# A hybrid encoder layer's FFN: weight loads set ahead of frame loads, frame loads one pair at a time, form stores on another queue, spare blocks for the last forms, later transposes

## The chip, the core and the metric

The kernel runs on one core of one Trainium2 chip. The metric is the device time of one execution in microseconds, as the median of several runs. The engines are named as the profile names them: PE (TensorE, matrix products) with its weight loads PEld, DVE (VectorE), ACT (ScalarE), POOL (GpSimd) and SP (SyncE, which here only issues DMAs). DMAs are issued from SP's queue and from POOL's.

## The reference

One layer of a streaming encoder is run over 512 prompt frames and 64 frames of a running stream, 576 frames in all, with a model width of 2048 and an inner width of the feed-forward part (FFN) of 5632. Everything is float32.

```python
hn = rmsnorm(x, g_norm1)
proj = hn @ w_in                        # split into q, k, v, gb, gc, hc
...                                     # stick-breaking attention and a short convolution
mix = concatenate([rmsnorm(o_attn, g_attn_out), rmsnorm(o_conv, g_conv_out)])
x = x + mix @ w_out
h2 = rmsnorm(x, g_norm2)
x = x + (silu(h2 @ w_gate) * (h2 @ w_up)) @ w_down
```

Outputs are the new x for prompt and sample frames, the new key and value rows, and the convolution's state.

## The kernel before

**Numbers.** A float32 product is made of three matmuls on float32r halves: weights and frames are split in a high part and a low part, and high x high, low x high and high x low are summed. A matmul takes a 128 x 128 weight tile as the stationary operand and 288 frames (half of the 576) as the moving one. A *step* is three such matmuls.

**Stages.** The first 985 us or so hold the norms, the input projection with attention and convolution, the output projection, and the first gate and up block of the FFN, computed plainly by `wide`: for each of two weight tiles (kk) four blocks (j, i) of 24 matmuls, j the column tile, i the half of the frames. The two halves of the frames lie in different tiles; the one in `b12h` and `b12l` shares its memory with the weight buffer `raw_b`, whose first loads therefore wait until `wide` has read these tiles for the last time.

**Units of seven products.** The rest of the FFN is cut into *units*, each a product of 2 x 2 blocks computed with seven products instead of eight (a Strassen-Winograd scheme). Units 0 to 41 make gate and up for the feature pairs fp = 1 to 21; each has m = 8 steps per product. The units from NGU = 42 on are the down projection: the table `DOWN` lists *visits* (d, a, b), where d is one of eight output column pairs, and the pairs a to b of hidden features are added, m = b − a steps per product. The four accumulator blocks of a d are made at its first visit (`take_blocks`) and put out at its last.

**Weights.** `load_columns` (L1020) issues weight loads on SP whenever a buffer is free: the buffer A (`raw_a`) and B (`raw_b`) have two halves each, and a visit with m over 4 needs both halves of one of them. `prepare(n, p_)` splits the weight block of product p_ of unit n into one of four slots `whl`: a cast on ACT (L211), a subtraction on DVE (L212), and on DVE the sums of weights (L1082, L1094). After product 3 or 4 a buffer is free, and `prepare` calls `load_columns`.

**Running a product.** `run` multiplies (L1112), copies a partial result out of PSUM with ACT (`part`, L1122) and adds it up on DVE and POOL (L1137, L1142, L1144). For gate and up, `finish` (L959 to L966) makes silu(gate) x up and `put_forms` makes the seven *forms* of a feature pair, the frame side of the down projection. Each form is split by `put_form` into a tile with tag `hl` (two buffers) and stored to `hid_dram` by a DMA on POOL (L924): 22 x 7 = 154 stores of 288 KB.

**Frames of the down projection.** `load_pair` brings one feature pair (7 forms, 2 MB) from `hid_dram` back into one of seven places, on SP: one DMA (L1236, tiles `h_s` or `t`), or seven of 288 KB (L1228, tile `t`) for two of the places. `turned` says after which product of the last up unit the pairs 0 to 6 are called, and `down_calls` after which visit the later ones are: as soon as the pair that holds a place is used by all eight d. Several pairs can be called at once: 7 to 10 behind one visit, 11 to 13 behind another.

**Output.** At a d's last visit `store_y` spawns a coroutine per block: it waits for 4 steps of the product loop, transposes the block on PE into PSUM (`pot`, L1257), copies it back with DVE (L1259) and ACT (`obs`, two buffers, L1261), waits 5 more steps and issues the stores on SP (L1248, L1250, L1264).

**Order.** `order` lists the products of all units, two units woven into each other. The main loop calls `prepare` of the product three places ahead (`AHEAD = 3`), then `run`, then `load_pair` for what is due. From the last up unit on (NGU − 1) ACT, DVE, SP and POOL keep the program's order; ahead of it a scheduler sets the order of their instructions. SP, ACT, DVE, POOL and PE each work in order: an instruction that waits holds all behind it.

```python
if k_ + AHEAD < len(order):
    prepare(*order[k_ + AHEAD])
run(n, p_)
for p in turned.get((n, p_), calls[n - NGU] if n >= NGU and p_ == 4 else ()):
    load_pair(p)
```

Of the kernel before, what the change touches and what calls it, by code (L numbers as in the profile page):

```python
# [10 lines left out]
F32 = mybir.dt.float32  # L11
F32R = mybir.dt.float32r
# [29 lines left out]


DOWN = (
# [5 lines left out]
)  # L50


# [41 lines left out]
def tile_hybrid_stream_step(  # L94
# [743 lines left out]
    def h2(kt, i):  # L838
        if i == 0:
            return h2a[kt]  # L840
        return b22s[kt // 2] if kt % 2 else (b12h[:, kt // 2, :], b12l[:, kt // 2, :])
# [47 lines left out]
    def ps_tile(name):  # L889
        turn[0] += 1  # L890
        if turn[0] % 2:
            return ps_pj.tile([P, HALF], F32, tag="pj", name=name)
        return ps_z.tile([P, 512], F32, tag=f"z{turn[0] // 2 % 3}", name=name)[:, :HALF]
# [23 lines left out]
    gates = {}  # L917
    hid = {}

    def put_form(fp, n, src):  # L920

        t = tmp.tile([P, 2, HALF], F32R, tag="hl", name="form")
        split(t[:, 0], t[:, 1], src)
        nc.gpsimd.dma_start(out=hid_dram[fp][2 * n - 2 : 2 * n].rearrange("f p t -> p f t"), in_=t.bitcast(F32))  # L924

    def put_forms(fp, c, i):

# [23 lines left out]
    def finish(kind, fp, c, i, ps, part=None):  # L951

        a, b = HALVES[i]
        if kind == "gate":
            s = gates[c, i] = tmp.tile([P, HALF], F32, tag="r" if i else "y", name="gs")
        else:
            s = tmp.tile([P, HALF], F32, tag="sq", name="ut") if c == i else h2pool.tile([P, HALF], F32, tag="hx", name="ux", bufs=2)
        if part is None:
            nc.vector.tensor_tensor(out=s, in0=ps, in1=R2[:, a:b], op=ALU.mult)  # L959
        else:  # L960
            nc.vector.tensor_tensor(out=s, in0=ps, in1=part, op=ALU.add)  # L961
            nc.vector.tensor_tensor(out=s, in0=s, in1=R2[:, a:b], op=ALU.mult)
        if kind == "gate":
            nc.scalar.activation(out=s, in_=s, func=AF.Silu)
            return
        nc.vector.tensor_tensor(out=s, in0=s, in1=gates.pop((c, i)), op=ALU.mult)  # L966
        hid.setdefault(fp, {})[c, i] = s
        put_forms(fp, c, i)

    def wide(kind, hold=None):  # L970

        pss = {}
        for kk in range(2):
            whi, wlo = next_weight()
            for j in range(2):
                for i in range(2):
                    if kk == 0:
                        pss[j, i] = ps_tile("pw")
                    for k in range(8):
                        xh, xl = h2(8 * kk + k, i)  # L980
                        for n, (w_, x_) in enumerate(((whi, xh), (wlo, xh), (whi, xl))):
                            mm(pss[j, i], w_[:, k, j * P : (j + 1) * P], x_,
                               start=(kk == 0 and k == 0 and n == 0), stop=(kk == 1 and k == 7 and n == 2))
                        pipe.tick()
                    if kk == 1:
                        finish(kind, 0, j, i, pss[j, i])
            if hold and kk == 0:
                hold()

# [203 lines left out]

    def take_blocks(d):

        if d == 0:
            down["z"] = h2pool.tile([P, 6, HALF], F32, tag="z", name="acc_z")
        if d in (0, 3):
            four = [down["z"][:, q, :] for q in (range(4) if d == 0 else range(4, 6))]
            if d:  # L1200
                ax = down["pool"].tile([P, 2, HALF], F32, name="ax")
                four += [ax[:, q, :] for q in range(2)]
        elif d < 3:
            pool, tag = (tpool, "t12z") if d == 1 else (ypool, f"y{NP - 1}")
            t = pool.tile([P, 4, HALF], F32, tag=tag, name=f"acc{d}")
            four = [t[:, q, :] for q in range(4)]
        elif d < 6:
            four = [pool.tile([P, HALF], F32, tag=tag, name=f"acc{d}", bufs=2)
                    for pool, tag in (((tmp, "y"), (tmp, "r")) if d == 4 else ((tmp, "sq"), (h2pool, "hx")))
                    for _ in range(2)]  # L1210
        else:
            pool, tag = (tmp, "hl") if d == 6 else (rpool, "R")
            two = [pool.tile([P, 2, HALF], F32, tag=tag, name=f"acc{d}", bufs=2) for _ in range(2)]
            four = [t[:, q, :] for t in two for q in range(2)]
        for q, ap in enumerate(four):
            acc[d, q // 2, q % 2] = ap

    def add_residual(d):
        for c in range(2):
# [3 lines left out]
    def load_pair(p):  # L1223
        q = p % SLOTS
        if q in (3, 6):
            slots[p] = [t34[f][:, q // 6] for f in range(FORMS)]
            for f in range(FORMS):
                nc.sync.dma_start(out=slots[p][f].bitcast(F32),  # L1228
                                  in_=hid_dram[p][2 * f : 2 * f + 2].rearrange("f p t -> p f t"))
            return  # L1230
        if q in (2, 4):
            t = t12[:, 1 - q // 4].rearrange("p j f t -> p (j f) t")
        else:
            t = h2s[q // 5][:, SB * (q % 5) : SB * (q % 5 + 1), :]
        slots[p] = [t[:, 2 * f : 2 * f + 2, :] for f in range(FORMS)]
        nc.sync.dma_start(out=t.bitcast(F32), in_=hid_dram[p].rearrange("f p t -> p f t"))  # L1236

    def store_y(n, c, i):

        d = UNITS[n][1]  # L1240
        src, cs, f0 = acc[d, c, i], slice((2 * d + c) * P, (2 * d + c + 1) * P), HALVES[i][0]
        r = HALF - 2 * P

        def put(f, ap):

            rows, n_p = ap.shape[0], max(min(TP - f, ap.shape[0]), 0)
            if n_p:
                nc.sync.dma_start(out=yp[f : f + n_p, cs], in_=ap[:n_p])  # L1248
            if n_p < rows:
                nc.sync.dma_start(out=ys[f + n_p - TP : f + rows - TP, cs], in_=ap[n_p:])  # L1250

        def work():
            yield 4
            po = misc("pot")[:, : 3 * P]
            for q in range(3):
                w = min(P, HALF - q * P)
                nc.tensor.transpose(po[:w, q * P : (q + 1) * P], src[:, q * P : q * P + w], ident)  # L1257
            ob = src[:, : 2 * P].rearrange("p (i c) -> p i c", c=P)
            nc.vector.tensor_copy(out=ob, in_=po[:, : 2 * P].rearrange("p (i c) -> p i c", c=P))  # L1259
            obs = down["pool"].tile([r, P], F32, tag="obs", name="obs", bufs=2)  # L1260
            nc.scalar.copy(out=obs, in_=po[:r, 2 * P :])  # L1261
            yield 5
            if i == 0:
                nc.sync.dma_start(out=yp[: 2 * P, cs].rearrange("(i p) c -> p i c", p=P), in_=ob)  # L1264
            else:
                put(f0, ob[:, 0, :])
                put(f0 + P, ob[:, 1, :])
            put(f0 + 2 * P, obs)

        pipe.spawn(work())  # L1270


    turned = {(NGU - 1, 2): (0, 1), (NGU - 1, 6): (2,), (NGU - 1, 7): (3,), (NGU - 1, 5): (4,),
              (NGU - 1, 3): (5,), (NGU - 1, 4): (6,)}
    mode = ExitStack()
    AHEAD = 3
    for k_ in range(AHEAD):
        prepare(*order[k_])
    for k_, (n, p_) in enumerate(order):
        if (n, p_) == (NGU - 1, 1):  # L1280
            mode.enter_context(tc.manual_schedule(engines={mybir.EngineType.Activation, mybir.EngineType.DVE,
                                                           mybir.EngineType.SP, mybir.EngineType.Pool}))
            down["pool"] = tc.alloc_tile_pool(name="dpool", bufs=1, reuse_waits="tile", side="left")
        if k_ + AHEAD < len(order):
            prepare(*order[k_ + AHEAD])
        run(n, p_)
        for p in turned.get((n, p_), calls[n - NGU] if n >= NGU and p_ == 4 else ()):
            load_pair(p)
        if p_ == 2:
            for d in residual.get(n, ()):  # L1290
                add_residual(d)
    pipe.flush()
    mode.close()
    down["pool"].release()
# [35 lines left out]
```

## Time and profile before

| | |
|---|---|
| median of 3 runs | 2501.8 us (2500.9 to 2502.32) |
| the profiled execution | 2507.3 us, its span 2505.6 us |
| granted TensorE clock, mean | 0.991 of full speed |
| PE busy | 2442.1 us, 97% of the span |
| DVE busy | 1752.2 us, 70% |
| ACT busy | 1075.8 us, 43% |
| POOL busy | 348.1 us, 14% |
| moved by DMA | 336.51 MB, 134 GB/s as a mean |

The profile is of one execution, and its times count from the start of the span. In rows of an engine's timeline the columns are the start and the length in us, the engine, the line of the kernel, the operation, what is written from what is read, the shape, how often, and in square brackets how long the engine sat idle before it and what released it. `A <- B: 9.6, 3, 4.6` in a list of waits says that A waited for B 9.6 us in total, 3 times, 4.6 us at most. A DMA row with a median at its end gives the KB of one transfer and the microseconds from issue to landing.

### The profile page before, as it was taken

The page shows a single profiled execution, that of the slowest core. Times are in us where ns is not written, and L with a number is a line of the kernel's source. Part 1 is how long each engine was busy: PE and PEld are TensorE (multiplying, and loading weights), DVE is VectorE, ACT ScalarE, POOL GpSimd, SP SyncE. Part 2 cuts the span into 40 slices and gives each one's busy share as a digit, 9 for nine tenths or more (in the row PEclk, how much of TensorE's full clock was granted, in tenths as well). Part 3 has the DMA queues.
Part 4 walks back from the last instruction along what each step waited for, and adds up shares of the span by engine and source line. Part 5 has one row for each costly group of instructions (what it writes and reads, how often), then busy time and mean ns, then how long its engine had stood idle before and what let it go on. Part 6 is the DMA issues. An engine that isn't in the chain of part 4 may idle for free. (4 is left out here: it accounts for less than half of the span.)

```text
span 2505.6 us, 44203 instructions
## 1 busy us (share of the span) xinstructions
PE 2442.1 (97%) x18137; PEld 2425.9 (97%) x18137; DVE 1752.2 (70%) x2701; ACT 1075.8 (43%) x1917; POOL 348.1 (14%) x490
## 2 busy tenths in 40 slices
PE   8999999999999999999999999999999898999997
PEld 8999999999999999999999999999999898999897
DVE  7766666353345557888888888888887777777775
ACT  5655565231132345444444444444443443344333
POOL 2111010110020120001011010110101003421211
PEclk9999999999999999999999999999999899999999
DMA  8232323222242333444445444454447637765532
GB/s 260 82 96 86 90 78 88 75 85 85 85 160 85 101 129 117 134 134 137 133 149 154 132 135 136 149 153 129 137 137 245 217 124 202 213 185 187 175 109 66
DMA packets 436339, 336.51 MB, mean 134 GB/s; under 512 B 10222, under 2 KB 418920, under 8 KB 436136
## 3 DMA queue, kind: packets, MB, share of 16 engines
q1 hardware_dynamic: 419208, 283.53, 37.6%
q0 software_dynamic: 16928, 50.15, 6.2%
q8 instruction: 142, 2.33, 0.4%
q14 instruction: 61, 0.50, 0.1%
HBM read 269.33 MB, written 64.31 MB: 133 GB/s over the span
## 5 line engine op out<-in xcount | busy, mean ns | idle before, releaser
L1112 PE MATMUL psy<-t,whl 128*128 128x288 f32 x2916 | 445.4, 298 | 11.4 <-ACT part L1122 9.6
L203 PE MATMUL pj<-xhi,whi 128*128 128x288 f32 x1504 | 451.7, 300 | 0.0
L203 PE MATMUL pj<-xlo,whi 128*128 128x288 f32 x1504 | 445.9, 297 | 1.7 <-DVE xlo L337 1.7
L203 PE MATMUL pj<-xhi,wlo 128*128 128x288 f32 x1504 | 445.5, 296 | 0.0
L1112 PE MATMUL psy<-h_s,whl 128*128 128x288 f32 x2724 | 419.4, 298 | 16.4 <-ACT part L1122 15.7
L1112 PEld LDWEIGHTS psy<-t,whl 128*128 128x128 f32 x2916 | 410.0, 191 | 14.2 <-ACT part L1122 10.8
L1112 PEld LDWEIGHTS psy<-h_s,whl 128*128 128x128 f32 x2724 | 383.6, 191 | 18.8 <-ACT part L1122 17.0
L1112 PE MATMUL psw<-t,whl 128*128 128x288 f32 x2592 | 380.9, 297 | 0.0
L212 DVE TENSOR_TENSOR whl<-raw_a,whl 128x1024 fp32r<-128x1024 f32 (+5 forms) x288 | 303.0, 1052 | 83.2 <-ACT whl L211 81.9
L1112 PEld LDWEIGHTS psw<-t,whl 128*128 128x128 f32 x2592 | 358.8, 190 | 0.0
L211 ACT CAST whl<-raw_a 128x1024 fp32r<-128x1024 f32 (+5 forms) x288 | 255.3, 894 | 142.4 <-DVE raw_a L1082 50.2
L203 PEld LDWEIGHTS pj<-xlo,whi 128*128 128x128 f32 x1504 | 285.1, 190 | 2.0 <-DVE xlo L337 2.0
L203 PEld LDWEIGHTS pj<-xhi,whi 128*128 128x128 f32 x1504 | 285.4, 190 | 0.4
L203 PEld LDWEIGHTS pj<-xhi,wlo 128*128 128x128 f32 x1504 | 285.3, 190 | 0.5 <-DVE wlo L167 0.2
L212 DVE TENSOR_TENSOR whl<-raw_b,whl 128x1024 fp32r<-128x1024 f32 (+5 forms) x198 | 195.2, 987 | 96.1 <-ACT whl L211 94.9
L211 ACT CAST whl<-raw_b 128x1024 fp32r<-128x1024 f32 (+5 forms) x198 | 163.2, 835 | 190.1 <-issue 72.7
L166 ACT CAST whi<-raw_a 128x1024 fp32r<-128x1024 f32 (+1 forms) x138 | 140.0, 1031 | 232.7 <-PE pj L203 95.8
L924 POOL DMA_DIRECT2D hid_dram<-form x154 | 112.5, 731 | 903.0 <-DVE form L212 756.2
L1122 ACT COPY part<-psy 128x288 f32<-128x288 f32 x243 | 96.8, 398 | 236.1 <-PE psy L1112 234.6
L167 DVE TENSOR_TENSOR wlo<-raw_a,whi 128x1024 fp32r<-128x1024 f32 (+1 forms) x132 | 160.2, 1226 | 24.0 <-ACT whi L166 22.7
L1112 PE MATMUL psx<-h_s,whl 128*128 128x288 f32 x1122 | 168.8, 299 | 6.0 <-DVE gs L961 6.0
L1112 PEld LDWEIGHTS psx<-h_s,whl 128*128 128x128 f32 x1122 | 157.4, 192 | 6.2 <-issue 6.2
(357 smaller groups left out, 3700.9 us busy)
## 6 DMA issues: line engine op xcount, KB each, us to landing
raw_a<-in_w_in_dram SPq DMA_DIRECT2D x47, 1024.0 KB, 5.6
hid_dram<-form POOLq DMA_DIRECT2D x154, 288.0 KB, 2.8
raw_a<-in_w_gate_dram SPq DMA_DIRECT2D x23, 1024.0 KB, 5.8
raw_a<-in_w_up_dram SPq DMA_DIRECT2D x23, 1024.0 KB, 6.0
raw_b<-in_w_gate_dram SPq DMA_DIRECT2D x21, 1024.0 KB, 7.1
raw_b<-in_w_up_dram SPq DMA_DIRECT2D x21, 1024.0 KB, 7.3
h_s<-hid_dram SPq DMA_DIRECT2D x10, 2016.0 KB, 12.6
raw_a<-in_w_out_dram SPq DMA_DIRECT2D x16, 1024.0 KB, 5.4
```

The source lines that it names most:

```text
L166: nc.scalar.copy(out=hi[:, a:b], in_=raw[:, a:b])
L167: lo_eng.tensor_tensor(out=lo[:, a:b], in0=raw[:, a:b], in1=hi[:, a:b].bitcast(F32), op=ALU.subtract)
L203: mm(ps, w_[:, k, csl], x_[:, k, a:b], start=(k == 0 and n == 0), stop=(k == nk - 1 and n == 2))
L211: nc.scalar.copy(out=hi, in_=src)
L212: (lo_eng or nc.vector).tensor_tensor(out=lo, in0=src, in1=hi.bitcast(F32), op=ALU.subtract)
L924: nc.gpsimd.dma_start(out=hid_dram[fp][2 * n - 2 : 2 * n].rearrange("f p t -> p f t"), in_=t.bitcast(F32))
L1112: mm(ps, whl[:, w_, j, :], x_, start=(start and j == 0 and q == 0), stop=(j == len(xs_) - 1 and q == 2), skip_group_check=True)
L1122: nc.scalar.copy(out=t, in_=st["y"])
```

## The change

- `AHEAD` goes from 3 to 4, and `run` now comes ahead of `prepare` in the main loop; `load_pair` still comes last.
- Pairs that are due go into a list. One is issued at a time, and only when enough steps have passed since the last: 8 for the pairs 0 and 1, 16 for the other ones in the last gate and up units, `PACE` = 20 in the down projection.
- Form stores go to SP's queue for all feature pairs but the last. The last pair's stay on POOL's, and its forms 5, 7, 6 and 4 are put into four spare blocks (`ax`, two of `t`, one of `z`), which `take_blocks` uses as accumulators later, instead of the `hl` tiles.
- `wide` runs its four blocks with the other half of the frames (i = 1) first.
- The table `DOWN` is another one, with 38 visits instead of 39. The last visits of the eight d have m = 5, 5, 3, 5, 3, 3, 4, 3; before they had 7, 7, 5, 3, 3, 3, 4, 6.
- `store_y` waits for 9 steps instead of 4 ahead of its transposes.

```diff
 DOWN = (
-    (0, 0, 3), (1, 0, 4), (2, 0, 4), (3, 0, 4), (0, 3, 7), (4, 0, 4), (5, 0, 4), (6, 0, 4), (7, 0, 7), (1, 4, 7),
-    (2, 4, 7), (3, 4, 8), (4, 4, 9), (5, 4, 9), (6, 4, 9), (0, 7, 10), (1, 7, 11), (2, 7, 12), (7, 7, 11), (3, 8, 13),
-    (4, 9, 15), (0, 10, 15), (5, 9, 16), (6, 9, 16), (1, 11, 16), (7, 11, 16), (2, 12, 17), (3, 13, 18), (1, 16, 19),
-    (5, 16, 19), (6, 16, 19), (0, 15, 22), (4, 15, 22), (2, 17, 22), (1, 19, 22), (5, 19, 22), (6, 19, 22), (3, 18, 22),
-    (7, 16, 22),
+    (0, 0, 3), (1, 0, 4), (2, 0, 4), (0, 3, 7), (3, 0, 4), (4, 0, 4), (5, 0, 4), (6, 0, 6), (7, 0, 5), (1, 4, 7),
+    (2, 4, 7), (3, 4, 8), (4, 4, 9), (6, 6, 10), (5, 4, 10), (7, 5, 11), (0, 7, 12), (1, 7, 12), (2, 7, 14),
+    (3, 8, 14), (4, 9, 15), (5, 10, 16), (0, 12, 17), (6, 10, 17), (7, 11, 17), (1, 12, 18), (2, 14, 19),
+    (3, 14, 19), (5, 16, 19), (4, 15, 19), (0, 17, 22), (6, 17, 22), (2, 19, 22), (7, 17, 22), (3, 19, 22),
+    (4, 19, 22), (1, 18, 22), (5, 19, 22),
 )
...
+    spare = []
     def put_form(fp, n, src):
-        t = tmp.tile([P, 2, HALF], F32R, tag="hl", name="form")
+        if fp == NFP - 1 and n > 3:
+            t = spare.pop(0)()
+        else:
+            t = tmp.tile([P, 2, HALF], F32R, tag="hl", name="form")
         split(t[:, 0], t[:, 1], src)
-        nc.gpsimd.dma_start(out=hid_dram[fp][2 * n - 2 : 2 * n].rearrange("f p t -> p f t"), in_=t.bitcast(F32))
+        q = nc.gpsimd if fp == NFP - 1 else nc.sync
+        q.dma_start(out=hid_dram[fp][2 * n - 2 : 2 * n].rearrange("f p t -> p f t"), in_=t.bitcast(F32))
...
-            for j in range(2):
-                for i in range(2):
+            for i, j in ((1, 0), (1, 1), (0, 0), (0, 1)):
...
+    def spare_tile(name, q):
+        if name not in down:
+            pool, n, tag = {"z": (h2pool, 6, "z"), "t": (tpool, 4, "t12z"), "ax": (down["pool"], 2, "ax")}[name]
+            down[name] = pool.tile([P, n, HALF], F32, tag=tag, name=f"acc_{name}")
+        return down[name][:, 2 * q : 2 * q + 2, :].bitcast(F32R)
+
+    for name, q in (("ax", 0), ("t", 0), ("t", 1), ("z", 2)):
+        spare.append(lambda name=name, q=q: spare_tile(name, q))
...
         def work():
-            yield 4
+            yield 9
...
-    AHEAD = 3
+    PACE = 20
+    pairs = []
+    since = PACE
+    AHEAD = 4
...
+        run(n, p_)
         if k_ + AHEAD < len(order):
             prepare(*order[k_ + AHEAD])
-        run(n, p_)
-        for p in turned.get((n, p_), calls[n - NGU] if n >= NGU and p_ == 4 else ()):
-            load_pair(p)
+        pairs += turned.get((n, p_), calls[n - NGU] if n >= NGU and p_ == 4 else ())
+        since += UNITS[n][3]
+        if pairs and since >= (PACE if n >= NGU else NP if pairs[0] < 2 else 2 * NP):
+            load_pair(pairs.pop(0))
+            since = 0
```

More of the change, by code (lines that the diff above doesn't have):

```diff
@@ L974, in wide @@
             whi, wlo = next_weight()
-            for j in range(2):
-                for i in range(2):
[L977 to L986, printed above, removed]
+            for i, j in ((1, 0), (1, 1), (0, 0), (0, 1)):
+                if kk == 0:
+                    pss[j, i] = ps_tile("pw")
+                for k in range(8):
+                    xh, xl = h2(8 * kk + k, i)
+                    for n, (w_, x_) in enumerate(((whi, xh), (wlo, xh), (whi, xl))):
+                        mm(pss[j, i], w_[:, k, j * P : (j + 1) * P], x_,
+                           start=(kk == 0 and k == 0 and n == 0), stop=(kk == 1 and k == 7 and n == 2))
+                    pipe.tick()
+                if kk == 1:
+                    finish(kind, 0, j, i, pss[j, i])
             if hold and kk == 0:
@@ L1194, in take_blocks @@
     def take_blocks(d):
-        if d == 0:
-            down["z"] = h2pool.tile([P, 6, HALF], F32, tag="z", name="acc_z")
         if d in (0, 3):
@@ L1200, in take_blocks @@
             if d:
-                ax = down["pool"].tile([P, 2, HALF], F32, name="ax")
-                four += [ax[:, q, :] for q in range(2)]
+                four += [down["ax"][:, q, :] for q in range(2)]
         elif d < 3:
-            pool, tag = (tpool, "t12z") if d == 1 else (ypool, f"y{NP - 1}")
-            t = pool.tile([P, 4, HALF], F32, tag=tag, name=f"acc{d}")
+            t = down["t"] if d == 1 else ypool.tile([P, 4, HALF], F32, tag=f"y{NP - 1}", name=f"acc{d}")
             four = [t[:, q, :] for q in range(4)]
@@ L1291, in tile_hybrid_stream_step @@
                 add_residual(d)
+    assert not pairs
     pipe.flush()
```

## The prediction

> **What bounds the kernel now.** I read the page's first section, then busy time by stretches of the span, then TensorE's waits, and at each stretch that loses time the timelines of the engine waited for and of SP's queue.
>
> ```profile
> span 2505.6 us, 44203 instructions
> PE 2442.1 (97%) x18137; PEld 2425.9 (97%) x18137; DVE 1752.2 (70%) x2701; ACT 1075.8 (43%) x1917; POOL 348.1 (14%) x490
> ```
> ```profile
> 985.00:1020.00 35.00, 28.21 (x190) 27.77 (x188) 26.33 (x34) 12.63 (x19) 4.22 (x6) 0.90 0.57 169
> 1020.00:1930.00 910.00, 910.00 (x6828) 910.00 (x6827) 755.85 (x1031) 415.93 (x629) 102.36 (x141) 1.00 0.48 144
> 1930.00:1960.00 30.00, 17.46 (x114) 16.99 (x113) 15.28 (x32) 7.71 (x18) 4.07 (x6) 0.77 1.08 373
> 1960.00:2070.00 110.00, 110.00 (x827) 110.00 (x826) 83.24 (x135) 52.75 (x103) 6.00 (x6) 1.00 0.44 142
> 2070.00:2100.00 30.00, 22.91 (x155) 22.23 (x154) 19.79 (x30) 10.01 (x20) 9.47 (x10) 0.89 0.82 242
> 2100.00:2180.00 80.00, 76.19 (x549) 74.66 (x548) 64.26 (x89) 30.91 (x59) 37.11 (x42) 0.98 0.82 207
> ...
> 2340.00:2390.00 50.00, 42.91 (x291) 41.35 (x290) 35.42 (x52) 18.11 (x34) 9.38 (x9) 0.93 0.36 114
> 2390.00:2500.00 110.00, 98.21 (x714) 93.46 (x712) 72.88 (x126) 39.32 (x93) 18.17 (x21) 0.98 0.29 84
> ```
>
> The columns are the length, the busy time and count of PE, weight loads, DVE, ACT and POOL, the granted clock, the DMA share and GB/s. TensorE is the bound: from 1020 to 1930 us it has no gap, and 6828 matmuls in 910 us make 7.503 per us, which I take as the full rate. The number of steps is the same in both kernels (3584 steps of three matmuls in the seven-product part; I summed m over all units and products), so the change can only win time that TensorE now loses. A stretch loses its length less its matmuls / 7.503: 985 to 1020 us 35 − 190/7.503 = 9.7; 1930 to 1960 us 14.8; 2070 to 2100 us 9.3; 2100 to 2180 us 6.8; 2340 to 2390 us 11.2; 2390 to 2500 us 14.8. Together 66.6 us is the most there is to win here. The losses exceed the waits below because the granted clock falls after a wait (0.77 to 0.93 in these rows).
>
> ```profile
> PE psy L1112 <- ACT part L1122: 26.1, 7, 12.2
> PE pot L1257 <- DVE acc L1142: 8.4, 6, 4.1
> PE psx L1112 <- DVE gs L961: 6.0, 1, 6.0
> ...
> PE psy L1112 <- DMA t<-hid_dram: 0.4, 1, 0.4
> ```
>
> TensorE's waits, with total, times and longest. It almost never waits for data by DMA itself. It waits for PSUM space that ACT's copies must free (`part`), for DVE, and for transposes queued too early (`pot`). The change works on what holds ACT and DVE.
>
> **Part 1, the first unit (wide order, spare blocks, stores).**
>
> ```profile
> ACT form L211 <- DMA hid_dram<-form: 9.6, 3, 4.6
> ```
> ```profile
> 984.86 0.37 SPq L1020 DMA_DIRECT2D raw_b<-in_w_gate_dram  x1
> ```
> ```profile
> 1000.76 5.38 PE L1112 MATMUL psx<-h_s,whl 128*128 128x288 f32 x21 [5.96 <-DVE gs L961]
> ```
>
> ACT waits three times for a form store to leave its two buffers while two weight loads run beside it; DVE stands behind ACT, and TensorE behind DVE for 5.96 us, then runs at the slow clock (5.38 us for 21 matmuls, where full rate gives 2.8). The new order of the four blocks ends the reading of the half that holds `raw_b` two blocks earlier: 2 x 24 matmuls / 7.503 = 6.4 us, so the load leaves at about 978.5 instead of 984.86 and most of it is done before the forms come. About 2.5 us of the 9.7 stay: gain 7, bounds 4 and 9.
>
> The Trainium skill's page "DMA: Bandwidth & Descriptors", section "Queues, rings and completion order", says that each DMA engine takes turns packet by packet between the queues with work; stores moved from POOL's queue into SP's, behind loads, lose their turn. By that rule the first store would wait for all of the load ahead, and the gain here would be the lower bound, 4, and the sum 3 less.
>
> **Part 2, stores of the other units.** Their number is unchanged, 147 of 154 stores going to SP.
>
> ```profile
> 1522.95 0.37 SPq L1020 DMA_DIRECT2D raw_a<-in_w_up_dram  x1
> ```
> ```profile
> 1523.70 0.72 POOL L924 DMA_DIRECT2D hid_dram<-form  x1 [20.98 <-DVE form L212]
> 1531.35 0.73 POOL L924 DMA_DIRECT2D hid_dram<-form  x1 [6.92 <-DVE form L212]
> 1536.22 0.73 POOL L924 DMA_DIRECT2D hid_dram<-form  x1 [4.15 <-DVE ux L932]
> ```
> ```profile
> raw_b<-in_w_up_dram SPq DMA_DIRECT2D x1, 1024.0 KB, 8.7
> ```
>
> The worst store of a unit leaves 0.75 us behind a weight load. If it lands 8.7 us after that load's issue (the slowest landing in this stretch), it is home at 1531.7, and its buffer is wanted by the form that is stored at 1536.22: some 3.5 us to spare. The other way round, a store on SP that waits for DVE holds the loads behind it; in program order the loads stand where they stand now in time, and a weight loaded here is used 22 us later or more (steps between its place in the program and its first use, at 0.4 us). So 0 for all of it; the cover is ACT's idle time. If that cover went, a wait of 1 us in each of 20 units would cost 20.
>
> **Part 3, the order of prepare and run.** `AHEAD` 4 with run first gives prepare(k+3), run(k), prepare(k+4): the same order on ACT and DVE as before. The copies don't move against each other; what moves is that a weight load now stands ahead of the pair on SP. It is worth nothing by itself and its effect is counted in parts 4 and 5.
>
> **Part 4, the first pairs.**
>
> ```profile
> 1911.70 1.92 SPq L1236 DMA_DIRECT2D h_s<-hid_dram  x2
> ...
> 1929.94 8.72 SPq L1228 DMA_DIRECT2D t<-hid_dram  x7
> ```
> ```profile
> 1950.03 0.43 ACT L211 CAST form<-ux 128x288 fp32r<-128x288 f32 x1 [4.22 <-DMA hid_dram<-form]
> ```
> ```profile
> 1937.18 0.67 PE L1112 MATMUL psy<-t,whl 128*128 128x288 f32 x3 [0.35 <-DMA t<-hid_dram]
> ...
> 1951.22 1.81 PE L1112 MATMUL psy<-h_s,whl 128*128 128x288 f32 x6 [12.19 <-ACT part L1122]
> ```
> ```profile
> hid_dram<-form POOLq DMA_DIRECT2D x8, 288.0 KB, 6.0
> ```
>
> Here the DMA is full (373 GB/s in the row of 1930 to 1960), a store takes 6.0 us, ACT waits for it, and TensorE waits 12.19 us. Spare blocks take ACT's wait away: up to −14.8. But pair 2, which lands just in time now (the wait of 0.35 us at 1937.18), goes out later: pairs 0 and 1 go one after the other, and three weight loads (1 MB each) stand ahead of pair 2 instead of one. Ahead of and in pair 2 there are then 3 pairs of 2.06 MB, 3 x 1.05 MB and some 2 MB of stores = 11.4 MB; at 0.36 to 0.37 MB/us from the first pair's issue (6.4 us behind the start of the last up unit, which is at about 1907) it lands 38 to 41 us behind that start, where it is wanted at 29.6 (74 steps of 0.4 us). So a stall of about 10 us takes the old one's place, with the slow clock behind it. Gain 1, bounds −4 and +10.
>
> **Part 5, the paced pairs and the new table.**
>
> ```profile
> 2064.23 11.03 SPq L1228 DMA_DIRECT2D t<-hid_dram  x7
> 2076.55 0.37 SPq L1020 DMA_DIRECT2D raw_b<-in_w_down_dram  x1
> ```
> ```profile
> 2087.23 0.72 ACT L211 CAST whl<-raw_b 128x640 fp32r<-128x640 f32 x1 [8.05 <-DMA raw_b<-in_w_down_dram]
> ```
> ```profile
> 2088.31 1.09 PE L1112 MATMUL psy<-t,whl 128*128 128x288 f32 x3 [6.05 <-ACT part L1122]
> ```
> ```profile
> 2142.18 13.87 SPq L1228 DMA_DIRECT2D t<-hid_dram  x7
> 2157.84 0.37 SPq L1020 DMA_DIRECT2D raw_a<-in_w_down_dram  x1
> ```
> ```profile
> 2170.11 1.22 PE L1112 MATMUL psy<-h_s,whl 128*128 128x288 f32 x6 [3.06 <-ACT part L1122]
> ```
> ```profile
> 2355.39 2.53 PE L1112 MATMUL psy<-t,whl 128*128 128x288 f32 x9 [3.00 <-ACT part L1122]
> ```
> ```profile
> h_s<-hid_dram SPq DMA_DIRECT2D x10, 2016.0 KB, 12.6
> ```
>
> The chain reads backwards: TensorE waits for `part`, ACT's copy stands behind a weight cast that waits for its DMA, and that DMA was issued behind a pair's seven transfers, whose issue alone took 11.03 and 13.87 us because the queue was full. With one pair in flight and weights ahead of it the loads leave when their slot is free. Counting steps in the new table, every weight load has at least 10.0 us between its place and its need (before, 8.4 us at the load behind the wait at 2355.39). So 2070 to 2100 us keeps about 1.7 of 9.3 (gain 7.6, bounds 5 and 9), 2100 to 2180 keeps 1 of 6.8 (gain 5.8, bounds 3 and 6.8), and 2340 to 2390 keeps 2.5 of 11.2 (gain 8.7, bounds 4 and 11). Against it: pairs 11 and 14 to 18 have only 11.2 to 11.6 us from place to first use, where a pair takes 12.6 us in the row above, in company. Alone, at the 0.37 MB/us that the full DMA moves, 2.06 MB is 5.6 us and a start, so I expect them in time and set aside 4 us (bounds 0 and 10).
>
> **Part 6, the output.**
>
> ```profile
> 2453.01 0.26 ACT L1261 COPY obs<-pot 32x128 f32<-32x128 f32 x1 [5.41 <-DMA out_dram<-obs]
> ```
> ```profile
> 2454.78 0.87 PE L1257 MATMUL pot<-ident,acc 128*128 128x128 f32 x3 [4.09 <-DVE acc L1142]
> ```
> ```profile
> 2501.82 0.26 ACT L1261 COPY obs<-pot 32x128 f32<-32x128 f32 x1 [1.31 <-DVE acc L1259]
> ```
>
> A transpose that is ready too early stops TensorE, since it is in order. Waiting 9 steps instead of 4 gives DVE 5 x 0.4 = 2.0 us more per output, which covers the waits of 1 to 2 us; the 4.09, set by an `obs` store behind a weight load, shrinks but stays. I keep 6 of 14.8. In exchange the last blocks' transposes fall behind the last product: three turns of three transposes, DVE copies and their stores, where before one was left (0.64 us of waiting at its transpose). I set 2 us. Gain 6.8, bounds −2 and +13.
>
> **The sum.** 7 + 0 + 0 + 1 + 7.6 + 5.8 + 8.7 − 4 + 6.8 = 32.9, rounded to 32. The profiled execution took 2507.3 us (its span and 1.7 around it), 5.5 above the median of 2501.8 of the runs; the losses are in the program's order, so they are taken off the median alike: 2507.3 − 32 = 2475.3 with a profile, 2470 as the median.
>
> **Rivals.** (a) The stall at the first pairs goes too, because the loads come faster than I count: another 12 us, 2458. For it: ACT's cause is really removed. Against: 11.4 MB at the measured rate. (b) Output gives nothing and the first pairs cost 6 more: 32 − 7 − 7 = 18, 2484. For it: DVE is busy for 66 and 71% of the last two stretches as a mean over products, denser beside an output, and outputs crowd into 31 steps' worth of last visits, where 38 held them before. (c) Slower: the paced pairs come late. Place: pairs 6, 11 and 14 to 18, seven of them, each stops TensorE at the first product of its unit. It decides from a landing of 16 us on: 16 − 11.4 = 4.6 and some slow clock, 5.2 each, times 7 = 36, which eats the gain before the 4 set aside; at 18 us it is 7 x 7.2 = 50, less 37 = 13 slower, 2515. For it: pairs now take 12.6 us in the middle. Against: they come three and four at a time there, and one at a time later. (d) The change does not do what it says: as part 3 shows, the copies do not move at all; if the late loads too stay where the slots' freeing puts them, only the first unit's 7 us are won, and what the output wins goes to the tail, 2495.
>
> **How the numbers follow.** My forecast 0.55, (a) 0.13, (b) 0.20, (c) 0.08, (d) 0.04. The bounds of the parts add to far ends that won't come together; the range goes from (a) with a good output, 2452, over (b) with both of its terms at the bound, to 2494, and leaves out (c), (d) and a little of the other cases. A measurement of this kernel tells 0.2%, about 5 us, from no change. Faster by more: 0.55 + 0.13 + 0.20 and a part of (d) = 0.89; same 0.03; slower 0.08.
>
> **What would show it.** Right: no wait of ACT for `hid_dram<-form` after the first unit; a TensorE wait for `t<-hid_dram` of about 10 us soon after 1930, in place of the one for `part`; loads in the down part issued with no seven-transfer group of over 5 us ahead; `pot` waits under 6 us in all; 1020 to 1900 still without a gap. Wrong: gaps in that long stretch (part 2), TensorE waits for a pair behind 2100 (rival c), or a `part` wait that stays at the old places (rival d).

## The result and the profile after

The changed kernel takes 2474.99 us as the median of 4 runs (2472.84 to 2477.99), against 2502.06 us for the kernel before beside it (4 runs, 2500.9 to 2503.66): a ratio of 0.9892 with a 95% interval of 0.9875 to 0.9909, or 27.1 us less. Forecast were 2470 us and 32 us less. The profiled execution took 2472.84 us, with a span of 2471.1 us: 34.5 us less than the span before.

Busy time by stretches of the span, in the columns of before (length, PE, weight loads, DVE, ACT, POOL, clock, DMA share, GB/s):

```profile
985.00:1020.00 35.00, 33.67 (x253) 33.43 (x252) 32.49 (x43) 15.83 (x26) 0.00 (x0) 1.00 0.40 124
1020.00:1900.00 880.00, 880.00 (x6603) 880.00 (x6602) 733.89 (x1004) 406.36 (x611) 0.00 (x0) 1.00 0.47 142
1900.00:1970.00 70.00, 59.34 (x434) 59.10 (x433) 45.07 (x77) 27.09 (x54) 5.33 (x7) 0.93 0.97 327
1970.00:2060.00 90.00, 90.00 (x682) 89.95 (x681) 69.26 (x111) 43.17 (x85) 8.85 (x9) 1.00 0.34 108
2060.00:2180.00 120.00, 116.27 (x865) 114.64 (x864) 98.27 (x122) 48.38 (x81) 50.87 (x57) 1.00 0.85 223
...
2180.00:2471.10 291.10, 272.06 (x2009) 266.67 (x2007) 210.09 (x318) 113.05 (x220) 52.41 (x57) 0.99 0.48 150
```

The same stretches of before, where they were cut in another way above:

```profile
1900.00:1970.00 70.00, 57.46 (x414) 56.99 (x413) 44.28 (x74) 26.23 (x50) 6.56 (x9) 0.90 0.95 320
...
2060.00:2180.00 120.00, 109.10 (x777) 106.88 (x776) 92.39 (x133) 46.34 (x90) 49.74 (x55) 0.96 0.84 229
2180.00:2506.00 326.00, 301.61 (x2202) 294.54 (x2200) 231.50 (x342) 124.57 (x237) 64.07 (x67) 0.98 0.46 142
```

The prediction's measure, length less matmuls / 7.503, gives what TensorE lost in each:

| stretch | lost before | lost after | won |
|---|---|---|---|
| 985 to 1020 (first unit) | 9.7 | 1.3 | 8.4 |
| 1020 to 1900 | 0 | 0 | 0 |
| 1900 to 1970 (first pairs) | 14.8 | 12.2 | 2.6 |
| 2060 to 2180 (late weights) | 16.4 | 4.7 | 11.7 |
| 2180 to the end of the span | 32.1 | 23.3 | 8.8 |

That is 31.5 us. The other 3 of the 34.5 are 17 and 5 more matmul records in the stretches to 985 and from 1970 to 2060 us. The first are no work of the change: a second profile of the kernel before has 7307 records to 985 us, the changed one 7306, the first one 7289. The 5 are a matter of the rate: between 1980 and 2050 us, without a gap in either, TensorE did 532 matmuls after and 527 before (last section).

TensorE's waits after, total, times and longest:

```profile
PE psy L1117 <- ACT part L1127: 12.2, 12, 2.4
PE psy L1117 <- DMA t<-hid_dram: 10.7, 1, 10.7
...
PE pot L1268 <- ACT obs L1272: 2.1, 2, 1.5
```

The wait for a pair, 0.4 us before, is the longest now. The wait for DVE in the first unit (6.0) is gone, and so is `pot` for DVE (8.4), but `part`, 26.1 in 7 waits before, is still there in 12 small ones. Where the long one stands, in TensorE's and in SP's timeline:

```profile
1936.82 1.09 PE L1117 MATMUL psy<-t,whl 128*128 128x288 f32 x3 [10.66 <-DMA t<-hid_dram]
```
```profile
1901.03 0.36 SPq L1247 DMA_DIRECT2D h_s<-hid_dram  x1
1910.23 0.37 SPq L1025 DMA_DIRECT2D raw_b<-in_w_down_dram  x1
1910.69 2.25 SPq L1247 DMA_DIRECT2D h_s<-hid_dram  x1
1913.70 2.79 SPq L1025 DMA_DIRECT2D raw_a<-in_w_down_dram  x1
1916.58 3.10 SPq L1025 DMA_DIRECT2D raw_b<-in_w_down_dram  x1
1919.77 3.03 SPq L1247 DMA_DIRECT2D t<-hid_dram  x1
```

The second pair (1910.69) goes 0.5 us behind a weight load that had to wait for its buffer until 1910.23; the third (1919.77) goes behind two more loads. It lands 17 us after its issue.

### The profile page after: what moved, and what is told of

Read it like the earlier page. It is cut to its first block, busy times and chain, and to the rows that moved or that the text cites. A ratio compares the mean times of both kernels' runs of the same rounds, so it can differ in the third digit from the quotient of the medians.

```text
span 2471.1 us, 44086 instructions
## 1 busy us (share of the span) xinstructions
PE 2426.1 (98%) x18137; PEld 2412.7 (98%) x18137; DVE 1746.7 (71%) x2686; ACT 1076.7 (44%) x1907; POOL 236.5 (10%) x340
## 5 line engine op out<-in xcount | busy, mean ns | idle before, releaser
L1117 PE MATMUL psy<-t,whl 128*128 128x288 f32 x2916 | 443.2, 297 | 16.9 <-DMA t<-hid_dram 10.7
L1117 PEld LDWEIGHTS psy<-t,whl 128*128 128x128 f32 x2916 | 406.5, 190 | 20.5 <-DMA t<-hid_dram 10.9
L212 DVE TENSOR_TENSOR whl<-raw_a,whl 128x1024 fp32r<-128x1024 f32 (+5 forms) x276 | 297.6, 1079 | 69.1 <-ACT whl L211 68.6
L211 ACT CAST whl<-raw_a 128x1024 fp32r<-128x1024 f32 (+5 forms) x276 | 248.7, 909 | 126.7 <-DVE raw_a L1087 45.7
L212 DVE TENSOR_TENSOR whl<-raw_b,whl 128x1024 fp32r<-128x1024 f32 (+5 forms) x204 | 203.2, 997 | 98.7 <-ACT whl L211 97.4
L211 ACT CAST whl<-raw_b 128x1024 fp32r<-128x1024 f32 (+5 forms) x204 | 168.8, 838 | 204.7 <-issue 73.8
L166 ACT CAST whi<-raw_a 128x1024 fp32r<-128x1024 f32 (+1 forms) x138 | 140.0, 1030 | 232.6 <-PE pj L203 95.8
L211 ACT CAST whl<-s 128x1024 fp32r<-128x1024 f32 (+5 forms) x80 | 70.1, 876 | 70.0 <-PE psw L1117 68.5
```

The lines of the kernel that those rows point to most:

```text
L166: nc.scalar.copy(out=hi[:, a:b], in_=raw[:, a:b])
L211: nc.scalar.copy(out=hi, in_=src)
L212: (lo_eng or nc.vector).tensor_tensor(out=lo, in0=src, in1=hi.bitcast(F32), op=ALU.subtract)
L1117: mm(ps, whl[:, w_, j, :], x_, start=(start and j == 0 and q == 0), stop=(j == len(xs_) - 1 and q == 2), skip_group_check=True)
```

## Experiments

Executions of one kernel scatter by up to 11 us here (2464.92 to 2476.05 for the changed kernel in one set), as much as most parts are worth. So the times are given with their ratio to the kernel before, and the verdicts are read from TensorE's loss in the stretch that an edit touches. That measure has limits too. Full rate has two levels (last section), which shifts a loss by up to 1 us per 100 us of stretch; and from 2180 us to the end two profiles of the same kernel differ by 0.7 us (the changed kernel, 24.0 and 23.3) and by 2.7 us (the kernel before, 34.8 and 32.1). Each edit is made to the changed kernel.

**The changed kernel again.** 

> The changed kernel once more, as the base for the others on this chip. My theory: 2473 to 2477 us, with one TensorE wait of 10 to 11 us for the third frame pair near 1925 us and about 1 us lost in the first unit. A rival, that the gain hangs on the one execution that was profiled: 2485 or more.

Measured: 2470.98 us, ratio 0.9882 (0.9851 to 0.9912), 2 us under the range that was expected; the wait for the third pair is 9.9 us, and the first unit loses 1.4 us (254 matmuls, at the 7.565 per us of this execution). The gain does not hang on one execution.

**The old order of the four blocks.**

```diff
-            for i, j in ((1, 0), (1, 1), (0, 0), (0, 1)):
+            for j, i in ((0, 0), (0, 1), (1, 0), (1, 1)):
```

> The changed kernel with the old order of the four blocks. My theory (the early weight load wins the first unit): about 7 us slower than the changed kernel, TensorE waits about 6 us near 1000 us. The rival (the stores on the SP queue alone win it): within 1 us of the changed kernel.

**All form stores on POOL.**

```diff
-        q = nc.gpsimd if fp == NFP - 1 else nc.sync
+        q = nc.gpsimd
```

> The changed kernel with all form stores on the queue of POOL as before. My theory (the queue of a store is worth nothing once the load goes early): within 2 us of the changed kernel, the long stretch full either way. The rival (the move of the stores is what wins the first unit): about 8 us slower, the wait near 1000 us back. By the rule that queues take turns, stores on POOL come home sooner next to a load: up to 1 us faster.

**Both undone.** 

> The changed kernel with both the old order of the four blocks and all form stores on POOL. Undone alone, each cost about 2 us in the first unit. My theory (each covers for the other, together they won 8 us there): the loss between 985 and 1020 us is 8 to 10 us again, with a TensorE wait of about 6 us for DVE. The rival (they add): a loss of 4 to 6 us.

Measured: 2479.08 us, ratio 0.9909 (0.989 to 0.9927), for the old order; 2476.05 us, 0.9897 (0.9876 to 0.9918), for POOL's queue; 2482.01 us, 0.9908 (0.9889 to 0.9928), for both. The first unit in the three profiles, in that order:

```profile
985.00:1020.00 35.00, 31.96 (x237) 31.28 (x236) 31.27 (x40) 15.19 (x25) 0.00 (x0) 1.00 0.56 162
```
```profile
985.00:1020.00 35.00, 32.30 (x241) 31.82 (x240) 31.66 (x43) 15.67 (x25) 4.38 (x6) 1.00 0.42 127
```
```profile
985.00:1020.00 35.00, 28.53 (x202) 28.09 (x201) 26.89 (x35) 12.54 (x21) 3.65 (x5) 0.90 0.57 168
```

At 7.503 per us the first loses 3.4 us and the third 8.1. The second ran its full stretch at 7.566 (see the last section), and loses 3.1 by that rate. Against 1.3 in the changed kernel the parts are worth 2.1, 1.8 and together 6.8 us: each covers for the other. My 7 us for the order alone fell, and so did the rival that SP's queue does it alone. The median of the old order does lie 8.1 us above that of the changed kernel timed beside it (2470.98), near my 7, but the first unit accounts for only 2.1 of it, and the rest isn't shown to come from the edit. The third kernel's timeline has the old stop back:

```profile
998.42 4.44 PE L1117 MATMUL psx<-h_s,whl 128*128 128x288 f32 x21 [5.64 <-DVE gs L967]
```

Why either helps: with stores on POOL beside loads that leave late, a store takes up to 7.4 us (median 5.3). On SP's queue with the old order, the three stores issued ahead of the loads land in 2.2 to 2.7 us; for the three issued among the loads the profile shows no landing, and ACT waits 4.6 us for one of them. With the early loads most of the loads are over when the forms come: with stores on POOL the first store still takes 7.8 us beside two loads, while in the changed kernel it leaves ahead of the second load and lands in 3.2.

**Transposes after 4 steps.**

```diff
-            yield 9
+            yield 4
```

> The changed kernel with transposes after 4 steps instead of 9. My theory of the prediction (the later turn saves about 7 us net of a tail of 2): 7 us slower, TensorE waits for its transposes (pot) 10 to 14 us in all. The rival (the waits only change their name, from pot to part): within 2 us, with pot waits of about 10 us and part waits smaller by as much.

Measured: 2473.84 us, ratio 0.9885 (0.9865 to 0.9906). TensorE's waits from 2330 us to the end, first with 4 steps, then in the changed kernel:

```profile
PE pot L1268 <- DVE acc L1147: 6.9, 3, 5.2
PE pot L1268 <- DVE acc_z L1147: 2.1, 2, 1.0
PE psy L1117 <- ACT part L1127: 1.9, 3, 0.8
PE pot L1268 <- POOL acc_z L1149: 1.8, 1, 1.8
```
```profile
PE psy L1117 <- ACT part L1127: 9.4, 9, 2.4
PE pot L1268 <- ACT obs L1272: 2.1, 2, 1.5
```

The `pot` waits are 12.0 us with 4 steps (two rows of 0.6 aren't shown) and 2.1 with 9, but `part` goes from 1.9 to 9.4. From 2180 us to the end 24.3 us are lost (293.5 − 2020/7.503) against 23.3: the later turning is worth 1 us, which two profiles of one kernel may differ by. The rival was right.

**No pace.**

```diff
-        if pairs and since >= (PACE if n >= NGU else NP if pairs[0] < 2 else 2 * NP):
+        while pairs:
             load_pair(pairs.pop(0))
             since = 0
```

> The changed kernel, but every frame pair is issued as soon as it is due, behind the weight loads of its place. My theory (late weight loads behind several pairs made the stops near 2090, 2170 and 2355 us): the stops near 2090 and 2170 us come back, 7 to 13 us slower, less up to 3 us where the first pairs go earlier. The rival (the new table alone cured them, by giving weight loads more time): within 3 us of the changed kernel, no stop of over 1 us there.

Measured: 2480.54 us, ratio 0.9904 (0.9885 to 0.9923). The old stops are back; SP's timeline and TensorE's:

```profile
2045.26 11.04 SPq L1239 DMA_DIRECT2D t<-hid_dram  x7
2057.54 0.37 SPq L1025 DMA_DIRECT2D raw_b<-in_w_down_dram  x1
```
```profile
2070.29 1.09 PE L1117 MATMUL psy<-t,whl 128*128 128x288 f32 x3 [7.92 <-ACT part L1127]
...
2162.22 1.81 PE L1117 MATMUL psy<-h_s,whl 128*128 128x288 f32 x6 [2.82 <-ACT part L1127]
```

In the changed kernel the loads of that place stand ahead of the seven transfers, and the next load leaves long behind them:

```profile
2060.04 0.37 SPq L1025 DMA_DIRECT2D raw_b<-in_w_down_dram  x1
2060.47 1.84 SPq L1025 DMA_DIRECT2D raw_a<-in_w_down_dram  x1
...
2063.76 11.65 SPq L1239 DMA_DIRECT2D t<-hid_dram  x7
2084.97 0.37 SPq L1025 DMA_DIRECT2D raw_b<-in_w_down_dram  x1
```

So the pace doesn't shorten the seven issues (11.65 us); it puts them behind the loads. From 2060 to 2180 us the kernel without it loses 15.6 us (783 matmuls) against 4.7: the pace is worth 10.9 us there. But from 1900 to 1970 us it loses only 6.4 (477 matmuls) against 12.2, and waits 2.7 us for the third pair instead of 10.7. The pace takes 5.8 us there.

**The first three pairs without a pace.**

```diff
-        if pairs and since >= (PACE if n >= NGU else NP if pairs[0] < 2 else 2 * NP):
+        while pairs and (pairs[0] < 3 or since >= (PACE if n >= NGU else 2 * NP)):
```

> The changed kernel, but the first three frame pairs are issued without a pace. My theory (the 10 us wait near 1925 us is the third pair's late issue behind two more weight loads): the wait falls to 0 to 5 us, the kernel is 6 to 12 us faster. The rival (the DMA has too much to move in that time whatever the order): the wait is 8 us or more, or the fourth pair takes its place, and the kernel is within 3 us.

Measured: 2462.39 us, ratio 0.9839 (0.9816 to 0.9862). 1900 to 1970 us lose 6.4 us, and the wait for the third pair is 2.62 us. My theory held for the wait. The stretch gives 5.8 us; the median lies 12.6 us under that of the changed kernel, and the profiled execution (2470.48 us) only 2.4, so the time alone doesn't tell the size.

**prepare before run, three ahead.**

```diff
-    AHEAD = 4
+    AHEAD = 3
...
-        run(n, p_)
         if k_ + AHEAD < len(order):
             prepare(*order[k_ + AHEAD])
+        run(n, p_)
```

> The changed kernel with prepare of the product three ahead in front of run, as before, and all else changed. My theory (the copies do not move, and with one pair in flight the queue order of a pair and a load matters little): within 2 us of the changed kernel, the same waits. The rival (a load that stands behind a pair is what comes late): stops of 2 to 6 us for weights return in the down projection.

Measured: 2467.5 us, ratio 0.9852 (0.9831 to 0.9873). It is faster, which neither theory expected. SP's and TensorE's timelines:

```profile
1900.91 1.92 SPq L1247 DMA_DIRECT2D h_s<-hid_dram  x2
1910.11 0.37 SPq L1025 DMA_DIRECT2D raw_b<-in_w_down_dram  x1
1913.59 0.37 SPq L1025 DMA_DIRECT2D raw_a<-in_w_down_dram  x1
1914.06 3.27 SPq L1247 DMA_DIRECT2D t<-hid_dram  x1
```
```profile
1929.21 1.07 PE L1117 MATMUL psy<-t,whl 128*128 128x288 f32 x3 [3.17 <-DMA t<-hid_dram]
```

The second pair is again in front of the load that waits for its buffer, so it leaves at once with the first; the third leaves 5.7 us earlier. From 1900 to 1970 us 5.4 us are lost (485 matmuls): the new order costs 6.8 us there. From 2060 to 2180 us it loses 3.5 (874 matmuls), not more than the 4.7 of the changed kernel. So late weights are cured by the pace, and setting `prepare` behind `run` adds nothing to that.

**No spare blocks** (forms 5, 7, 6, 4 of the last pair in the two form tiles).

```diff
         if fp == NFP - 1 and n > 3:
-            t = spare.pop(0)()
+            spare.pop(0)()
+            t = tmp.tile([P, 2, HALF], F32R, tag="hl", name="form")
```

> The changed kernel without the spare blocks: the last pair's forms 5, 7, 6 and 4 go into the two form tiles. My theory (with the DMA full, ACT waits for stores again, but TensorE now waits for the third pair anyway): ACT waits for stores 5 to 10 us near 1930 us, the kernel is 0 to 4 us slower. The rival (the spare blocks are what wins the transition): 8 us or more slower.

Measured: 2477.39 us, ratio 0.9883 (0.9855 to 0.9911). ACT's waits between 1900 and 1960 us:

```profile
ACT form L211 <- DMA hid_dram<-form: 9.6, 2, 5.6
```

ACT waits 9.6 us again, and the stretch from 1900 to 1970 loses 14.3 us (418 matmuls) against 12.2. The blocks are worth 2.1 us while TensorE waits for the third pair anyway.

**The old table of visits.** The table `DOWN` of before, all else as changed. 

> The changed kernel with the table of visits of before, all else changed. My theory (the table is worth the stop at 2355 us, and little elsewhere): 5 to 9 us slower, with stops for weights only near 2355 us. The rival (the table is worth nothing, the order of loads does it all): within 3 us.

Measured: 2478.21 us, ratio 0.9901 (0.9877 to 0.9926). It loses 7.8 us from 2060 to 2180 (842 matmuls) and 28.9 from 2180 to the end (299.3 − 2029/7.503), 3.1 and 5.6 more than the changed kernel. The old stop is still there:

```profile
2331.09 1.46 PE L1117 MATMUL psy<-t,whl 128*128 128x288 f32 x9 [3.23 <-ACT part L1127]
```

By the profile the table is worth 8.7 us, and the pace does not cure this stop; from 2060 to 2180 TensorE has no wait of over 1.1 us here. The medians (2478.21 against 2474.99 us) don't tell my theory from the rival.

**First pairs without a pace, and four `obs` tiles.** The output's small waits begin at ACT:

```profile
2415.75 0.26 ACT L1272 COPY obs<-pot 32x128 f32<-32x128 f32 x1 [3.61 <-DMA out_dram<-obs]
2415.91 0.38 ACT L1127 COPY part<-psy 128x288 f32<-128x288 f32 x1
```
```profile
2416.34 0.66 PE L1117 MATMUL psy<-h_s,whl 128*128 128x288 f32 x3 [2.39 <-ACT part L1127]
```

The edit of the first three pairs, and:

```diff
-            obs = down["pool"].tile([r, P], F32, tag="obs", name="obs", bufs=2)
+            obs = down["pool"].tile([r, P], F32, tag="obs", name="obs", bufs=4)
```

> The changed kernel with the first three frame pairs issued without a pace and four obs tiles instead of two. My theory (what is left in the output is ACT held by obs behind weight loads on SP, and part behind obs): no wait of ACT for out_dram<-obs, part waits fall from 12 us to 4 to 8 us, 2456 to 2460 us, 2 to 5 us under the kernel with the first pairs alone. The rival (DVE is the bound in the last visits): part waits stay over 9 us, within 2 us of that kernel.

Measured: 2459.55 us, ratio 0.9825 (0.9808 to 0.9842). ACT waits for no `out_dram<-obs` (13.1 us in 4 waits with the first pairs alone), TensorE's waits for `part` from 2330 us on fall from 9.1 to 6.4 us (over the whole span from 13.7 to 10.2), and 18.6 us are lost from 2180 to the end (281.2 − 1970/7.503) against 23.7 with the first pairs alone. The profiles give 5.1 us; the intervals of the two timed ratios overlap. This kernel beats both the kernel before and the changed one.

**The kernel before again.** 

> The kernel before once more, for a second profile. In the long stretch between 1020 and 1900 us full rate was 752 to 753 matmuls per 100 us in some executions and 758 to 759 in others, over the same code. If that spread is the chip's and not the kernel's, the kernel before shows either of the two here, and its time beside its losses follows the level (7 us between them); if it belongs to the changed order, the kernel before keeps 753.

Measured: 2503.08 us, ratio 1.0002 (0.9991 to 1.0013), with 752 matmuls per 100 us and the same waits. The question on the spread stays open (last section).

## Why the prediction came out as it did

The sign and the range were right, and the median lies 5 us above the forecast.

- *First unit*, forecast 7 of 9.7, measured 8.4. The load left as early as forecast: at 976.22 us, where 978.5 was stated and the 17 records further ahead make up 2.3. The size held, the reason only in part: the order was to give 7 alone, and is worth 2.1 with the stores on SP. The Trainium skill's rule on queues that take turns (page "DMA: Bandwidth & Descriptors", section "Queues, rings and completion order") would have had the move of the stores cost 3 us. It won 1.8 alone: the store that left ahead of the second load landed in 3.2 us on SP's queue, against 7.8 on POOL's.
- *Other stores*: 0 forecast, 0 measured; 880 us without a gap. But the sign that was named, no wait of ACT for a form store after the first unit, did not hold, and the 3.5 us to spare were not there in every unit: between 1020 and 1895 us ACT waits for form stores 35 times, 32.2 us in all, 2.6 at most (before 21 times, 29.3 us). As part 2 says, ACT's idle time covers it. At the last pair, where before it waited 11.2 us in 3 waits, there is none.
- *Order of prepare and run.* That ACT's and DVE's order is the same, and that only SP's changes, held. "Worth nothing by itself" did not: it costs 6.8 us at the first pairs. The prediction had the mechanism in part 4 (three loads ahead of pair 2), but not that taking back this one edit would undo it.
- *First pairs*: forecast a stall of about 10 us in place of 12.19 and a gain of 1; measured 10.66 us and 2.6. The order of loads and pairs was read rightly; that the size fits so well is in part luck. The 11.4 MB at 0.36 to 0.37 MB/us, 6.4 us behind the start of the unit, make 37 to 38 us and not 38 to 41, so a stall of about 8; and from 1901 to 1937 us the DMA moved only 325 GB/s. Rival (a) stated that this stall would vanish; it did not, and with the first pairs sent sooner most of it does.
- *Late weights*, 2060 to 2180 us: forecast 7.6 + 5.8 less the 4 set aside, measured 11.7. TensorE waits for no pair behind 2100 us, so the 4 were not needed, and rival (c) fell. The cause was right in that loads behind seven transfers come late; what puts the loads ahead is the pace, not the new order in the loop. The sign, no group of over 5 us ahead of a load, held only in effect: groups of 11.65 and 9.43 us are still there, but the next load leaves 9.6 and 6.9 us after them.
- *The end*, from 2180 us: forecast 8.7 + 6.8 = 15.5, measured 8.8 (11.5 against the second profile of the kernel before). This is the step that failed in size, by 6.7 us, and both of its terms were too large. The stop at 2355.39 was given the whole row of 2340 to 2390 less 2.5; but that row also holds two waits of the output:

```profile
2371.09 0.55 PE L1257 MATMUL pot<-ident,acc_z 128*128 128x128 f32 x3 [2.62 <-POOL acc_z L1144]
...
2388.56 0.55 PE L1257 MATMUL pot<-ident,acc_z 128*128 128x128 f32 x3 [1.08 <-DVE acc_z L1142]
```

From 2180 to 2365 us, ahead of these, the kernel before loses 6.1 us (185 − 1342/7.503), and the changed kernel up to 2330, where its output hasn't begun, nothing:

```profile
2180.00:2330.00 150.00, 150.00 (x1127) 150.00 (x1126) 109.47 (x142) 60.74 (x94) 23.60 (x27) 1.00 0.62 199
```

So the stop gave about 6 of its 8.7, and the output with its tail (26.0 lost before, 23.3 after) 2.7 of its 6.8, the term "keep 6 of 14.8" less a tail of 2. The half of rival (b) by which the output gives nothing came nearer. The later turn is worth 1 us, because ACT's `obs` copy stands ahead of `part`: what TensorE no longer waits for at `pot` it waits for at `part`. The tail behind the last product is some 2.5 us longer (8.0 against 5.5), near the 2 that were set.

The terms add up to 32.9, which the prediction rounds to 32. That the 31.5 of the table is so near is luck: the end fell 6.7 short, and the first unit, the first pairs and the 4 us set aside for nothing made up for most of it. The median's gain of 27.1 is smaller than the profile's 34.5 because the profiled execution of before lay 5.2 us above the median of 2502.06, and that of after 2.2 us below; the assumption that both medians would follow the profiles alike is what made 2470 of 2475. Why single executions differ is not settled.

## What to carry to other kernels

A queue that works in order is paced by its waits, not by the place of an instruction in the program: a load that waits for its buffer holds back every transfer behind it that could already go, so put what is ready first, and space out only the transfers that flood the queue. Undo each part of a change alone and in pairs: here two parts covered for each other, and one cost as much as another won. When an early wait of an engine is moved, ask what stands next in order on the engine that it used to hide.

## What the runs showed of the hardware

Full rate has two levels. Between 1030 and 1130 us TensorE did 752 or 753 matmuls in 12 of the 14 profiled executions, and 758 or 759 in two (the changed kernel again, and all stores on POOL), at a granted clock of 1.00 in both; over 880 us that is 6603 and 6657 matmuls, some 7 us. It is time and not lost records: from the first to the last of the 19 loads `raw_a<-in_w_up_dram` behind 1030 us 806.4 us pass in the changed kernel, and 799.7 in those two. The kernel that ran at the faster level here ran at the slower one in its first profile, so code alone doesn't decide it, and the level can change within an execution: from 2180 to 2330 us the kernel with the first pairs alone, at 752 above, did 1137 matmuls, and the changed kernel again, at 759 above, 1127. Of 27 executions of the kernel before that were timed beside the experiments, three took 2494.67, 2495.23 and 2496.94 us and the others 2500.84 or more; none of the three was profiled, so that they ran at the faster level isn't shown. The cause is open.

A wait of 2.82 us was enough for the matmuls behind it to run slowly (6 in 1.81 us at 2162.22, where full rate needs 0.8), while 3 behind a wait of 2.62 us took 0.67 us, where other groups of 3 take 0.55 to 0.56. How soon the slow clock sets in varies: behind 3.23 us the first 9 matmuls took 1.46 us (2331.09, old table; full rate needs 1.2), yet from 2331 to 2335 us only 21 were done, at a granted clock of 0.68, where full rate makes 30.
